# Expert stage of a transformer block: first two matrices behind the preceding third one, empty slots' rows out of bounds

## The chip, the cores and the metric

The kernel runs on one core of a Trainium2 chip. The metric is the device time of one execution in microseconds (us). TensorE is called PE, VectorE DVE, ScalarE ACT, GpSimd POOL; SyncE (SP) only issues transfers here.

## What is computed

A block with two attentions (not touched here) and a mixture of 32 experts over 512 tokens of width 1024, all in float32. Each token goes to two experts, so there are 1,024 rows of expert work. The part that matters, cut from the reference:

```python
top_v, top_i = lax.top_k(elog, TOP_K)                  # 2 experts for each token
yb = (silu(xc @ w1[e]) * (xc @ w3[e])) @ w2[e]         # w1, w3: 1024x512; w2: 512x1024
y = yb[dest] * sw[:, None]
out = segment_sum(y, stok, num_segments=T)             # a token's two rows are added
x = x + out
```

The weights w1, w3 and w2 of all experts are 32 x 3 x 2 MB = 201 MB, and each is read once.

## The kernel before

The expert stage (`moe`) handles the 32 experts as 16 pairs, p = 0 to 15. Each expert has 64 slots (`C`), so a pair fills the 128 partitions: the first expert has partitions 0 to 63, the second 64 to 127, and an expert's rows stand at the front of its 64 slots. The other slots are empty.

For one pair, `ffn` does this. PE multiplies the gathered tokens with w1 (32 matmul instructions, L1185) and with w3 (32 more). ACT takes the silu of the first result, DVE multiplies it by the second (L1203), PE transposes the product (4 instructions, L1205), ACT copies the transposed tile back (hT, L1208), and PE multiplies it with w2 (32 instructions, L1223, two blocks of 512 columns). ACT and DVE scale the two blocks into y by the router's weight, and POOL adds the 128 rows of y (4 KB each) into a buffer in HBM, obuf, by an indirect accumulating transfer (L1254). Its row numbers come from `slot_tables`: a filled slot names its token's row, 0 to 511; an empty slot on partition p names a row of its own behind them, 512 + p. obuf has 640 rows for that.

After each odd pair there is extra PE work for the next two pairs: small tables (16 instructions, L1154) behind w3, and the gathering of their tokens (64 instructions, L1050 and L1051) behind the transposes. `blocks`, some 20 small DVE instructions which prepare the rare overflow loop, is traced after pair 0 and shares the buffer tagged hg with silu's result.

The last pair is different: its w2 comes in blocks of 256 columns, and each block's rows are spread to the tokens by matmuls (pcb, L1245 and L1246) and added to X, the content of obuf, which POOL loads (L1318) into the two buffers that held w2's first two column blocks; then the result goes out.

Weights are loaded by SP alone (`load`, L898) in a fixed order, w1, w3, w2 of pair 0, then of pair 1, and so on, as transfers of 1 MB (198 transfers; the last pair's w2 comes in six of 512 KB and four of 256 KB). They land in a ring of 38 half-megabyte places, so transfer j can only be issued when transfer j-19 has been used up by PE, and a transfer that waits holds back all behind it.

PE's order is chosen by the scheduler when the kernel is built, within the dependencies and the orders written by hand. One of these is in `ffn`: from the middle of w1 (k = 4, `KF`) on, a pair's w1 goes behind the last w2 matmul of the pair before (`self.third`). The first half of w1, and w3, carry no such order. `self.third` is empty for pair 0 and set back in the overflow loop.

Of the kernel before, what the change touches and what calls it, by code (L numbers as in the profile page):

```python
# [20 lines left out]
mult, add, sub, eq = OP.mult, OP.add, OP.subtract, OP.is_equal  # L21

P = 128
T = 512
# [7 lines left out]
NEG = -1e30  # L32
NE = 32
EG = 8
KF = 4
C = 64
KS = 512
E0 = 8
# [31 lines left out]
class Kernel:  # L70
# [1033 lines left out]
    def moe(self):  # L1104
# [6 lines left out]
        def gather(base):  # L1111


            ns = base.shape[1]
            xT = wk.tile([P, KT, ns], F32, tag="xT", name="xT")
            sel = self.sel(ns)
            first = len(self.pgs) > 0
            for k2 in range(4):
                if first:
                    pg = self.pgs.pop(0)  # L1120
                else:
                    pg = ps.tile([P, 2, ns], F32, name="pg", tag="G", bufs=4)
                    for t in range(NT):
                        for k in (2 * k2, 2 * k2 + 1):
                            self.pick(pg, k, t, sel[t])
                for k in (2 * k2, 2 * k2 + 1):
                    src, gg = pg[:, k % 2, :], self.g2d[:, k:k + 1]
                    if k % 2:
                        s.activation(xT[:, k, :], src, AF.Copy, scale=gg)
                    else:  # L1130
                        v.tensor_scalar(xT[:, k, :], src, gg, None, op0=mult)
            return xT
# [5 lines left out]
        def token_rows(sel):  # L1138

            R = sel[0].shape[1]  # L1140
            sT = wk.tile([P, T], F32R, tag="sT", name="sT")
            pr = ps.tile([P, T], F32, name="pr", tag="Y")
            for t in range(NT):
                pe.transpose(pr[0:R, t * P:(t + 1) * P], sel[t].bitcast(F32), ident)
            s.copy(sT[0:R], pr[0:R])
            return sT
# [22 lines left out]
        def ffn(xT, cols, w, table, after=lambda: None, blocks=((0, 512), (512, 512)), sT=None, first=lambda: None, mid=lambda: None):  # L1169
# [8 lines left out]
            for name in ("w1", "w3"):  # L1178
                p = ps.tile([P, 512], F32, name="p" + name, tag="H")
                for k in range(KT):  # L1180
                    with ExitStack() as behind:
                        if name == "w1" and k == KF and self.third:
                            behind.enter_context(tc.issue_after(self.third))
                        for i in range(n):
                            end = pe.matmul(p[i * C:(i + 1) * C], xT[:, k, cols[i]], w(name, i, k),  # L1185
                                            start=k == 0, stop=k == KT - 1)
                after()
                ph.append(p)
# [27 lines left out]
            def outputs(c0, m):  # L1216
                o = c0 % 512
                if o == 0 and store:
                    y["h"] = wk.tile([P, 2, 512], F32R, tag="y" if c0 else "xT", name="yhl")
                p = ps.tile([P, m], F32, name="py", tag="Y")  # L1220
                for k in range(4):
                    for i in range(n):
                        e = pe.matmul(p[i * C:(i + 1) * C], hT[:, k, i * C:(i + 1) * C], w("w2", i, k, c0, m),  # L1223
                                      start=k == 0, stop=k == 3)
                self.third = e.ins
                if not store:
                    if c0:
                        e = v.tensor_scalar(yy[:, c0:c0 + m], p, ws, None, op0=mult)  # L1228
                    else:
                        e = s.activation(yy[:, c0:c0 + m], p, AF.Copy, scale=ws)  # L1230
                    self.evicted.append(e.ins)
                    return
                yh, yl = (y["h"][0:R, i, o:o + m] for i in range(2))
                s.activation(yh, p[0:R], AF.Copy, scale=ws[0:R])
                v.scalar_tensor_tensor(yl, p[0:R], ws[0:R], yh.bitcast(F32), op0=mult, op1=sub)
                return yh, yl
# [14 lines left out]
            if not store:  # L1251
                for b in blocks:
                    outputs(*b)
                g.indirect_dma_start(self.obuf, bass.IndirectOffsetOnAxis(ap=rows, axis=0), yy, None,  # L1254
                                     bounds_check=T + P - 1, compute_op=add)
                after()
                return
            done = None
# [8 lines left out]
        def overflow():  # L1267
# [3 lines left out]
            with tc.For_i(0, n, 1) as i:  # L1271
                e = nc.sync.value_load(oi[0:1, bass.ds(i, 1)], min_val=0, max_val=NE - 1)
                kb = wk.tile([P, 2], F32, tag="kb", name="kb")
                j = wk.tile([P, NB], F32, tag="kbj", name="kbj")
                v.scalar_tensor_tensor(j, iota16, self.octr, self.okey, op0=eq, op1=mult, accum_out=kb[:, 0:1])
                v.tensor_scalar(self.octr, self.octr, 1.0, None, op0=add)
                base = wk.tile([P, C], F32, tag="hg", name="obase")
                v.tensor_scalar(base, slot4[:, 0:C], kb[:, 0:1], -float((EG - 1) * KS), op0=add, op1=add)
                for t in range(NT):
                    self.select(t, base)  # L1280
                xT = gather(base)
                v.tensor_tensor(kb[:, 1:2], slotp, kb[:, 0:1], op=add)
                table, sT = slot_tables([(self.sel(C), kb[:, 1:2])])[0], token_rows(self.sel(C))

                ww, slot = {}, RA
                for name in ("w1", "w3", "w2"):
                    src = self.io[name][0][bass.ds(e, 1)].rearrange("o (p k) m -> p (o k m)", p=P)
                    for h in (0, 2):
                        t = self.ring1.tile([P, 2, 1024], F32, tag=f"w{slot}", name="wo")
                        nc.sync.dma_start(t.rearrange("p a b -> p (a b)"), src[:, 1024 * h:1024 * (h + 2)])  # L1290
                        ww[name, h], ww[name, h + 1] = t[:, 0], t[:, 1]
                        slot += 2

                def w(name, _, k, c0=0, m=512):
                    h, o = (k, c0) if name == "w2" else (k // 2, k % 2 * 512)
                    return ww[name, h][:, o:o + m]
                ffn(xT, (slice(0, C),), w, table, sT=sT)

        def pair_sel(p):
            c0 = p % 2 * 2 * C  # L1300
            return [x[:, c0:c0 + 2 * C] for x in self.sel(4 * C)]

        def tables(q):
            r = []
            for p in (2 * q, 2 * q + 1):
                kcol = wk.tile([P, 1], F32, tag="kcol", name="kcol", bufs=2)
                v.tensor_scalar(kcol, slotp, float(self.expert(p, 0) * KS), None, op0=add)
                r.append((pair_sel(p), kcol))
            return slot_tables(r)

        tabs, got, self.evicted, self.third = tables(0), [], [], None
        for p in range(NE // 2):
            last, odd = p == NE // 2 - 1, p % 2
            c0 = odd * 2 * C
            if last:
                self.X = [self.xpool.tile([P, 2, D], F32, tag=n, name="X") for n in ("c0", "c1")]
                for i, x in enumerate(self.X):
                    g.dma_start(x, self.obuf[2 * i * P:2 * (i + 1) * P].rearrange("(t p) m -> p t m", p=P))  # L1318
            elif odd:
                v.tensor_scalar(key, key, -float(KS), None, op0=add)  # L1320
                for t in range(NT):
                    self.select(t, slot4)

            def first():
                got.append(tables(p // 2 + 1))

            def mid():
                got.append(gather(slot4))
            ffn(xT, (slice(c0, c0 + C), slice(c0 + C, c0 + 2 * C)),
                lambda name, i, k, c0=0, m=512: self.weight(name, self.expert(p, i), k, c0, m), tabs[odd],  # L1330
                lambda: self.load(8), [(c, 256) for c in range(0, D, 256)] if last else ((0, 512), (512, 512)),
                token_rows(pair_sel(p)) if last else None, *((first, mid) if odd and not last else ()))
            if odd and not last:
                tabs, xT = got
                got.clear()
            if p == 0:
                self.blocks(ps, wk)
        overflow()

# [36 lines left out]
```

## Time and profile before

| | us |
|---|---|
| median of 3 runs | 1063.03 |
| lowest and highest | 1061.3, 1063.7 |
| profiled execution, its own time | 1062.07 |
| its span from first to last instruction | 1060.3 |
| PE busy | 965.3 |
| DVE, ACT, POOL busy | 478.4, 385.0, 229.9 |

The span is shown on the page in 40 slices of 26.5 us; a digit is a busy share in tenths. Attention fills the first half, the expert stage begins at about 555 us. "DMA share" is the mean busy share of the 16 DMA engines, and GB/s is what they moved. A row of the timeline gives start and duration in us, then engine, line, operation, names (out<-in), shape and count; in brackets the idle time before it and what ended it.

### The profile page before, as it was taken

To read this page: it belongs to the slowest core of one execution; us is meant where nothing else is said; L and a number is where in the kernel's file an instruction comes from. 1 tells how busy PE (TensorE), PEld (TensorE's weight loads), DVE (VectorE), ACT (ScalarE), POOL (GpSimd) and SP (SyncE) were. 2 spreads that over 40 slices of the span, in tenths; PEclk is the share of its full clock that TensorE was granted. 3 is DMA by queue.
4 is the path that set the end of the run, shared out by engine and by line. 5 is a ranking of instruction groups with operands and counts; after the bars stand their busy time and mean duration, and the time that the engine had idled before them with its cause. 6 is when DMAs were issued, how large, how long until landed. Compare 5 with 4: busy or idle time off the path is not lost.

```text
span 1060.3 us, 15524 instructions
## 1 busy us (share of the span) xinstructions
PE 965.3 (91%) x5718; PEld 682.9 (64%) x5718; DVE 478.4 (45%) x1469; ACT 385.0 (36%) x802; POOL 229.9 (22%) x378
## 2 busy tenths in 40 slices
PE   7799999999899999989999899999697987979886
PEld 7799989999678788879993535353262532626233
DVE  3868585574859889796471312112020120201002
ACT  5475565746856655654361111111010110101001
POOL 6444344314523232333230000000000000000000
PEclk9899999999999999999989899999898998989988
DMA  6322222112311211245879899999999999999995
GB/s 176 117 66 74 62 80 80 47 37 74 96 55 48 63 56 38 60 165 190 334 291 387 320 403 402 404 401 402 426 402 403 401 404 420 404 402 405 402 388 205
DMA packets 76510, 254.26 MB, mean 240 GB/s; under 512 B 11664, under 2 KB 46224, under 8 KB 52368
## 3 DMA queue, kind: packets, MB, share of 16 engines
q1 hardware_dynamic: 70304, 238.56, 57.9%
q0 software_dynamic: 2704, 9.96, 4.2%
q10 hardware_dynamic: 3424, 4.72, 1.2%
q8 instruction: 46, 0.75, 0.3%
q14 instruction: 32, 0.26, 0.1%
HBM read 240.64 MB, written 12.58 MB: 239 GB/s over the span
## 4 chain that ended last, share of the span: by engine, by line
PE 53%; DMA 31%; DVE 9%; ACT 3%; issue 1%; SPq 0%; POOL 0%; DVEq 0%; ACTq 0%; POOLq 0%
DMA w<-in_w_dram 29%; PE pw L1185 8%; PE py L1223 5%; PE pmm L92 5%; PE pmm L93 5%; PE pmm L94 5%; PE po L92 2%; PE po L94 2%; PE po L93 2%; PE pg L92 2%; PE pg L94 2%; PE pg L93 2%; PE pg L1050 2%; PE pg L1051 2%; PE pt L413 1%
## 5 line engine op out<-in xcount | busy, mean ns | idle before, releaser
L1185 PE MATMUL pw<-w,xT 128*64 128x512 f32 x1024 | 248.7, 611 | 46.9 <-DMA w<-in_w_dram 46.9
L314 POOL TENSOR_TENSOR wlo<-wraw,whi 128x256 fp32r<-128x256 f32 (+4 forms) x228 | 174.9, 799 | 219.1 <-ACT whi L312 208.8
L1185 PEld LDWEIGHTS pw<-w,xT 128*64 128x64 f32 x1024 | 83.2, 141 | 200.2 <-issue 185.1
L92 PE MATMUL pmm<-whi,hTh 128*128 128x256 f32 (+1 forms) x448 | 130.1, 293 | 3.7 <-ACT raw L480 2.6
L93 PE MATMUL pmm<-wlo,hTh 128*128 128x256 f32 (+1 forms) x448 | 130.1, 293 | 0.0
L94 PE MATMUL pmm<-whi,hTl 128*128 128x256 f32 (+1 forms) x448 | 127.4, 292 | 0.0
L1254 POOL DMA_INDIRECT obuf<-y,rows x15 | 23.5, 1570 | 455.3 <-DVE y L1228 455.3
L1223 PE MATMUL py<-w,hT 128*64 128x512 f32 x480 | 112.9, 603 | 1.4 <-ACT hT L1208 1.4
L1228 DVE TENSOR_SCALAR y<-py,ws 128x512 f32<-128x512 f32 x15 | 11.3, 751 | 191.1 <-PE py L1223 191.1
L1203 DVE TENSOR_TENSOR hg<-pw,hg 128x512 f32<-128x512 f32 (+1 forms) x19 | 16.4, 877 | 171.8 <-PE pw L1185 171.4
L92 PEld LDWEIGHTS pmm<-whi,hTh 128*128 128x128 f32 x448 | 85.5, 191 | 5.6 <-ACT raw L480 3.2
L93 PEld LDWEIGHTS pmm<-wlo,hTh 128*128 128x128 f32 x448 | 85.5, 191 | 2.0 <-issue 1.7
L94 PEld LDWEIGHTS pmm<-whi,hTl 128*128 128x128 f32 x448 | 84.1, 191 | 1.8 <-issue 1.7
L1223 PEld LDWEIGHTS py<-w,hT 128*64 128x64 f32 x480 | 37.4, 138 | 65.1 <-issue 61.3
L1208 ACT COPY hT<-pt 128x512 f32<-128x512 f32 x15 | 8.8, 586 | 178.7 <-PE pt L1205 178.7
L312 ACT CAST whi<-wraw 128x1024 fp32r<-128x1024 f32 (+4 forms) x70 | 64.7, 931 | 20.9 <-DMA wraw<-in_w_in_dram 6.7
L399 ACT ACTIVATE e<-pss,nm 128x128 f32<-128x128 f32 (+3 forms) x96 | 50.7, 531 | 49.8 <-DVE nm L395 36.9
L1050 PE MATMUL pg<-sel,hTh 128*128 128x256 f32 x256 | 65.7, 295 | 0.0
L1051 PE MATMUL pg<-sel,hTl 128*128 128x256 f32 x256 | 64.4, 290 | 0.0
L1200 ACT ACTIVATE hg<-pw 128x512 f32<-128x512 f32 x16 | 17.1, 1067 | 130.4 <-PE pw L1185 118.3
L395 DVE CUSTOM_DVE_ANT_0 pss<-pss,mask 128x128 f32<-128x128 f32 (+3 forms) x96 | 46.9, 496 | 18.4 <-PE pss L531 15.8
L92 PE MATMUL pg<-hTh,whi 128*128 128x512 f32 x128 | 50.8, 397 | 0.9 <-DVE cT L87 0.9
(349 smaller groups left out, 1902.4 us busy)
## 6 DMA issues: line engine op xcount, KB each, us to landing
w<-in_w_dram SPq DMA_DIRECT2D x188, 1024.0 KB, 21.3
wraw<-in_w_in_dram SPq DMA_DIRECT2D x38, 512.0 KB, 3.6
w<-in_w_dram SPq DMA_DIRECT2D x6, 512.0 KB, 11.3
wraw<-in_w_in_dram SPq DMA_DIRECT2D x8, 352.0 KB, 3.3
obuf<-X ACTq DMA_DIRECT2D x5, 512.0 KB, 10.8
wraw<-in_mla_w_ukv_dram SPq DMA_DIRECT2D x4, 512.0 KB, 4.2
wraw<-in_w_o_dram SPq DMA_DIRECT2D x4, 512.0 KB, 3.4
X<-in_x_dram SPq DMA_DIRECT2D x4, 512.0 KB, 5.0
```

The source lines that it names most:

```text
L92: self.pe.matmul(out, a[0], b[0], start=first, stop=False)
L93: self.pe.matmul(out, a[0], b[1], start=False, stop=False)
L94: self.pe.matmul(out, a[1], b[0], start=False, stop=last)
L312: s.copy(hi, raw)
L314: g.tensor_tensor(lo[:, k], raw[:, k], hi[:, k].bitcast(F32), op=sub)
L395: v.tensor_tensor_reduce(out=pss[:, 0:nk], in0=pss[:, 0:nk], in1=self.mask[:, 512 - nk:512], scale=-scale, scalar=3e38, op0=add, op1=OP.mi ...
L399: s.activation(e[:, 0:nk], pss[:, 0:nk], AF.Exp, scale=-1.0, bias=nm, accum_out=l[:, m:m + 1] if l0 is None or m else l0[qt])
L1050: self.pe.matmul(pg, self.h2h[:, t, k, :], sel, start=t == 0 and k % 2 == 0, stop=False, skip_group_check=True)
L1051: self.pe.matmul(pg, self.h2l[:, t, k, :], sel, start=False, stop=t == NT - 1 and k % 2 == 1, skip_group_check=True)
L1185: end = pe.matmul(p[i * C:(i + 1) * C], xT[:, k, cols[i]], w(name, i, k), start=k == 0, stop=k == KT - 1)
L1223: e = pe.matmul(p[i * C:(i + 1) * C], hT[:, k, i * C:(i + 1) * C], w("w2", i, k, c0, m), start=k == 0, stop=k == 3)
L1254: g.indirect_dma_start(self.obuf, bass.IndirectOffsetOnAxis(ap=rows, axis=0), yy, None, bounds_check=T + P - 1, compute_op=add)
```

## The change

Three edits. (1) The order by hand now holds from k = 0 on, and for w1 and w3 alike: a pair's first and second matrix go wholly behind the third of the pair before. (2) In the accumulating transfer the bound on row numbers is 511 in place of 639, and a number above it is no error: the rows of empty slots, 512 + p, are then out of bounds and left out. (3) `blocks` is traced after pair 1 in place of pair 0.

```diff
-KF = 4
@@ ffn
-                        if name == "w1" and k == KF and self.third:
+                        if k == 0 and self.third:
                             behind.enter_context(tc.issue_after(self.third))
@@ ffn, behind w2
                 g.indirect_dma_start(self.obuf, bass.IndirectOffsetOnAxis(ap=rows, axis=0), yy, None,
-                                     bounds_check=T + P - 1, compute_op=add)
+                                     bounds_check=T - 1, oob_is_err=False, compute_op=add)
@@ moe, loop over pairs
-            if p == 0:
+            if p == 1:
                 self.blocks(ps, wk)
```

## Rows read from the trace of the kernel before

**Rows 1.** The page's 40 slices: PE, DMA, rate.
```profile
PE   7799999999899999989999899999697987979886
...
DMA  6322222112311211245879899999999999999995
GB/s 176 117 66 74 62 80 80 47 37 74 96 55 48 63 56 38 60 165 190 334 291 387 320 403 402 404 401 402 426 402 403 401 404 420 404 402 405 402 388 205
```
**Rows 2.** A quiet window: engines' busy us, granted PE clock, DMA share, GB/s.
```profile
660.00:670.00 10.00, 10.00 (x57) 5.03 (x58) 4.02 (x12) 1.63 (x3) 0.00 (x0) 1.00 1.01 424
```
**Rows 3.** PE's waits, 557 to 1040 us: total us, times, longest.
```profile
PE pw L1185 <- DMA w<-in_w_dram: 46.9, 16, 9.2
PE pt L1205 <- DVE hg L1203: 5.4, 2, 4.2
PE py L1223 <- ACT hT L1208: 1.4, 2, 0.7
```
**Rows 4.** SP's waits, 440 to 1060 us: total us, times, longest.
```profile
SPq L898 <- DMA w<-in_w_dram: 336.4, 147, 4.6
SPq L898 <- PE py L1223: 31.5, 7, 14.5
```
**Rows 5.** PE's timeline, pairs 0 and 1.
```profile
557.11 17.39 PE L1185 MATMUL pw<-w,xT 128*64 128x512 f32 x80
574.43 0.66 PE L1205 MATMUL pt<-ident,hg 128*128 128x128 f32 x4
575.02 5.79 PE L1185 MATMUL pw<-w,xT 128*64 128x512 f32 x25
...
580.70 6.97 PE L1223 MATMUL py<-w,hT 128*64 128x512 f32 x30
...
599.64 1.12 PE L1205 MATMUL pt<-ident,hg 128*128 128x128 f32 x4 [4.16 <-DVE hg L1203]
```
**Rows 6.** Timeline of DVE, ACT and PE between w3 and w2 of pair 2.
```profile
631.10 1.06 DVE L1203 TENSOR_TENSOR hg<-pw,hg 128x512 f32<-128x512 f32 x1 [13.40 <-PE pw L1185]
...
634.67 0.59 ACT L1208 COPY hT<-pt 128x512 f32<-128x512 f32 x1 [9.72 <-PE pt L1205]
...
635.30 7.09 PE L1223 MATMUL py<-w,hT 128*64 128x512 f32 x32 [0.68 <-ACT hT L1208]
```
**Rows 7.** Windows around the hole in the transfers (columns as in rows 2).
```profile
576.00:583.00 7.00, 7.00 (x36) 2.54 (x34) 0.00 (x0) 0.00 (x0) 0.00 (x0) 1.00 0.92 382
583.00:590.00 7.00, 7.00 (x34) 2.60 (x30) 0.75 (x1) 0.69 (x1) 0.10 (x1) 1.00 0.35 118
...
595.00:601.00 6.00, 1.84 (x12) 1.75 (x12) 3.68 (x19) 1.25 (x2) 0.00 (x0) 0.67 1.04 328
601.00:608.00 7.00, 7.00 (x49) 7.00 (x49) 0.99 (x3) 1.33 (x3) 0.00 (x0) 0.79 1.01 427
```
**Rows 8.** The software DMA queue, 622 to 629 us: packets, MB, share of 16 engines.
```profile
q0 software_dynamic: 144, 0.52, 37.6%
```
**Rows 9.** PE's timeline, pairs 14 and 15.
```profile
1018.06 0.61 PE L1185 MATMUL pw<-w,xT 128*64 128x512 f32 x1 [1.77 <-DMA w<-in_w_dram]
...
1018.55 6.99 PE L1223 MATMUL py<-w,hT 128*64 128x512 f32 x30
...
1025.44 10.03 PE L1185 MATMUL pw<-w,xT 128*64 128x512 f32 x45
...
1038.85 2.81 PE L1223 MATMUL py<-w,free 128*64 128x256 f32 x24
```
**Rows 10.** SP's issue of the last 1 MB transfer, and landing times of it and its neighbours.
```profile
L898 SPq DMA_DIRECT2D w<-in_w_dram x1: 328/328/328, 1005.8 to 1005.8; - x1
...
DMA to landing us min/median/max: 18.6/19.1/19.6
```
**Rows 11.** Timeline of POOL and DVE: X at the end.
```profile
1041.96 1.54 POOL L1318 DMA_DIRECT2D X<-obuf  x2 [12.89 <-PE py L1223]
...
1047.45 1.29 DVE L1248 TENSOR_TENSOR X<-pcb,X 128x512 f32<-128x512 f32 x2 [1.69 <-DMA X<-obuf]
```

## The prediction

> **What bounds the kernel now.** I read the 40 slices first. The rate stands at 401 to 426 GB/s from slice 24 to slice 38, with the DMA engines at 9, while PE's digit drops to 6 and 7 in places [rows 1]. A quiet window gives the ceiling: 424 GB/s at a DMA share of 1.01 [rows 2]. So the expert stage runs at the pace of its weights. The waits say the same from both sides. PE waits for weights 16 times, 46.9 us in all [rows 3]; SP waits 336.4 us for its own earlier transfers, and only 31.5 us for places of w2 [rows 4]. Two places are not at that pace. Slices 20 to 23 hold 291, 387, 320 GB/s before the level is reached [rows 1]: there the ring is full and PE is late. And the last pair ends after its weights, as shown below. Anything saved in transfer time, in a hole of the transfers, or behind the last weight moves the end; what is saved or lost on PE in between does not, up to its waits.
>
>
> **The start: part 1, the order.** Before, PE does 80 matmuls in 17.39 us (w1 and w3 of pair 0, and 16 of pair 1's w1), the transposes, then 25 more of pair 1, and only then, to 587.7, pair 0's w2 [rows 5]. One matmul takes 17.39 / 80 = 0.217 us. The ring wants w2's places next: SP waits up to 14.5 us for them, the longest wait of all [rows 4], and the transfers have a hole. It costs (1 - 382/424) x 7 = 0.7 us in one window and (1 - 118/424) x 7 = 5.05 us in the next [rows 7], 5.7 us together.
> After the change w2 of pair 0 follows its own w1 and w3: 557.1 + 64 x 0.217 = 571.0; the multiplication, transposes and copy lie bare before it, 1.06 + 0.66 + 0.59 = 2.3 us [rows 5, 6]; 32 matmuls take 6.9 us. It ends at about 580.3, 7.3 us sooner, and the first places come free in its second half, at 579. The hole begins in the 576 to 583 window and holds until after 587, so it closes. Gain 5.7 us; the bounds are 0 (a later place is waited for instead) and 7.3.
>
> **The cover that is lost.** For each even pair the 2.3 us between w3 and w2 had matmuls of the next pair beside them (ahead of pair 2's w2 PE idled 0.68 us [rows 6]). Now PE stands still: 8 x 2.3 = 18 us at most. For odd pairs the tables and the gathering still lie there. Of the 18 us only pair 0's stands on the path (counted above); the others eat into 46.9 us of waiting [rows 3], so I cost them at nothing. Without that cover they cost 16 us. Behind w1 and w3, held back on PE's queue, wait silu and DVE's multiplication of the same pair, and SP's reuse of those places; w1's and w3's data arrive after w2's of the pair before in any case, so the new order is the order of arrival.
>
> **Part 2, the rows left out.** An accumulating transfer is 128 rows of 4 KB. Alone in a 7 us window, its queue shows 144 packets, 0.52 MB, 37.6% of the engines: 2.63 us of all 16 engines for one transfer [rows 8]. At 424 GB/s 0.52 MB would take 1.24 us, so an accumulating byte costs twice a plain one. There are 15 such transfers, 39.5 us. How many rows are empty: 1,024 rows of work over 16 pairs leave, for the first 15, about 960 of 1,920 slots; with the reference's router on its inputs I get 975 filled and 945 empty, 49.2%. If an empty row costs nothing and the rest spreads evenly, 15 x 2.63 x 0.492 = 19.4 us go. But a weight transfer has landed when its slowest engine is done, and filled slots stand at the front of each half of the partitions, so the engines may not be relieved alike; if one of them keeps all its rows, or if an empty row still makes its packet, nothing goes. No row of before shows which. Between 0 and 19.4 I take two thirds, 13 us: the average over engines is a row's figure, the loss to uneven sharing is not. That is 0.87 us for each transfer, 12.1 us for the 14 that lie ahead of the last pair's weights.
> [...]
> POOL's own time for the transfer isn't on the path; bounds 0.
>
> **Part 3, `blocks`.** It takes the buffer that silu of pair 1 wants: PE idles 4.16 us before pair 1's transposes [rows 5], and the clock falls to 0.67 and 0.79 for the 13 us around it [rows 7]. Behind pair 1 the DVE chain runs beside pair 2's w1 (6.9 us). It frees up PE at a time when the transfers are at their ceiling again (427 GB/s [rows 7]), so: nothing, bounds 0 and 4.
>
> **The end: part 1 once more.** Pair 14's w2 (30 matmuls from 1018.55) had to wait until 1018.06 for a first matmul on weights of pair 15, and then 45 matmuls of w1 and w3 run from 1025.44 to 1035.47 without a wait [rows 9]: PE is 10 us of work behind. The last of w3 was issued at 1005.8 and landed 18.6 to 19.6 us later, at about 1025 [rows 10]. In the new order pair 14's w2 is long done, and w3's second half, 16 x 0.217 = 3.5 us, ends at 1028.9 in place of 1035.5. From there on everything follows as before: two column blocks until 1041.66 [rows 9], then X is loaded into their places at 1041.96, and DVE adds from 1047.45 [rows 11]. Gain 6.6 us. Less: pair 14's accumulating transfer, which ran behind those weights, now comes ahead of them and delays them by what is left of it, 2.63 - 0.87 = 1.8 us. Net 4.8, bounds 0 (the clock falls behind a wait, as to 0.67 in a window with 4.16 us of it [rows 5, 7]; at half clock w3's second half takes 3.5 us more, and the rest likewise) and 6.6.
>
> **The sum**, against the profiled execution: 1062.07 - 5.7 - 12.1 - 4.8 = 1039.5. The median is 1.0 above that execution: 1040.
>
> **Rivals.**
> - *The rows are left out but no transfer time is.* Each empty row still makes a packet, or the fullest engine keeps all its rows. For it: filled rows stand close together. Against: the rows of one transfer are the only thing that its packets count. 1062.07 - 5.7 - (6.6 - 2.6) = 1052.4, so 1053 as a median.
> - *Only the rows count.* The order gives back what it gains: another place of the ring is waited for at the start, and X or the last column blocks bind at the end. For it: X's data is waited for, 1.69 us [rows 11]. 1062.07 - 13.0 = 1049.1, so 1050.
> - *PE becomes the bound (slower).* Every pair, not only the even ones, has a bare stretch, and the clock falls behind each as it did after the 4.16 us [rows 7]: 2.3 us plus some 2.2 us at half clock, 4.5 x 15 = 67.5 us, against 46.9 + 5.4 + 1.4 = 53.7 us that PE idles now [rows 3]; 1062 + 13.8 = 1076. It decides from 53.7 / 15 = 3.6 us a pair on. Against: odd pairs keep 9 us of other work there, and behind the gap of 0.68 us 32 matmuls took 7.09 us, full pace [rows 6].
> - *No difference*: hole, rows and tail all give back; 1063.
>
> **How the numbers follow.** Forecast 0.60, with its own range of 1030 (all of the 19.4 saved, 7.3 at the start) to 1046. No transfer time saved 0.22; only the rows 0.09; PE bound 0.06; no difference 0.03. The range takes in the first three: from 1029 to 1054, the 1053 with a little room. Faster by over 0.2% (2.1 us, about what a measurement of this kernel can tell from no change) are the first three, 0.91; within it 0.03; slower 0.06.
>
> **What would show each step.** After: no 118 GB/s window near 585, and no wait of SP for w2 of over 10 us; w2 of pair 0 ending near 580. The software queue with about 15 x 65 rows in place of 1,920, and its share of the engines near 2.5% in place of 4.2%; if the packets fall but the weights' pace between pairs doesn't, the engines are not relieved alike. PE's waits for weights in more and shorter pieces, and bare gaps of 2 to 3 us at even pairs only. At the end, w3's last matmul 3 to 4 us behind its landing. Wrong I would be above all if the queue's packets stay at their number, or if PE's waits vanish.

## The result, and the profile after

The changed kernel takes 1037.93 us (median of 4, 1036.11 to 1039.05) beside 1062.76 us of the kernel before on the same chip: 24.8 us less, ratio 0.9766 with a 95% interval of 0.9746 to 0.9785. The forecast was 1040. The profiled execution has 1039.05 us and a span of 1037.3 us.

The page's slices (25.9 us each), and its two main DMA queues (packets, MB, share of the 16 engines):

```profile
PE   7799999999989999999999999999998897987985
...
DMA  6422222122322112153697999999999999999996
GB/s 175 124 62 63 82 82 69 42 58 69 84 62 64 56 42 61 31 190 122 250 380 282 408 412 411 423 405 421 415 410 417 409 412 407 426 411 411 413 362 235
...
q1 hardware_dynamic: 70304, 238.56, 59.6%
q0 software_dynamic: 2704, 6.10, 2.5%
```

Against [rows 1] the level of 405 GB/s and more is reached at slice 23 (counted from 1) and holds to slice 38 without a hole, and PE's digit is 9 from slice 13 to 30. The software queue moves 6.10 MB; the page of before has 2704 packets, 9.96 MB and 4.2%. So the packets stay at their number, 3.86 MB go (945 rows of 4 KB are 3.87 MB), and 1.7% of the span, 18 us of all 16 engines.

Waits of PE (557 to 1040 us) and of SP (440 to 1060 us), to be read beside [rows 3, 4]: total us, times, longest.

```profile
PE pw L1184 <- DMA w<-in_w_dram: 17.1, 9, 3.6
PE pt L1204 <- DVE hg L1202: 9.6, 8, 1.2
PE py L1222 <- ACT hT L1207: 5.4, 8, 0.7
PE py L1222 <- DMA w<-in_w_dram: 3.1, 3, 1.3
...
SPq L897 <- DMA w<-in_w_dram: 295.6, 135, 4.3
SPq L897 <- PE py L1222: 39.2, 14, 13.3
SPq L897 <- PE pw L1184: 36.1, 20, 5.5
```

PE waits 20.2 us for weights where it waited 46.9, and stands bare in 8 pairs for 9.6 + 5.4 = 15.0 us: the cover that the even pairs lost. SP still waits up to 13.3 us for w2's places, but the transfers already issued cover that now. The start shows it (PE's timeline, then windows with columns as in [rows 7]):

```profile
557.78 13.95 PE L1184 MATMUL pw<-w,xT 128*64 128x512 f32 x64
572.96 0.66 PE L1204 MATMUL pt<-ident,hg 128*128 128x128 f32 x4 [1.22 <-DVE hg L1202]
574.29 8.78 PE L1222 MATMUL py<-w,hT 128*64 128x512 f32 x32 [0.68 <-ACT hT L1207]
...
576.00:583.00 7.00, 7.00 (x32) 2.21 (x30) 0.00 (x0) 0.69 (x1) 0.00 (x0) 0.86 1.01 421
583.00:590.00 7.00, 7.00 (x36) 2.35 (x34) 0.75 (x1) 0.00 (x0) 1.84 (x1) 1.00 1.00 401
```

In place of 80 + 25 matmuls ahead of pair 0's w2 [rows 5] there are 64, and 583 to 590 us holds 401 GB/s where it held 118. At the end (timeline of PE, issue and landing of the last 1 MB transfer, POOL and DVE; beside [rows 9 to 11]):

```profile
1003.47 8.78 PE L1184 MATMUL pw<-w,xT 128*64 128x512 f32 x30 [2.32 <-DMA w<-in_w_dram]
...
L897 SPq DMA_DIRECT2D w<-in_w_dram x1: 328/328/328, 987.6 to 987.6; - x1
...
DMA to landing us min/median/max: 20.9/20.9/20.9
...
1018.74 1.52 POOL L1317 DMA_DIRECT2D X<-obuf  x2 [22.75 <-DMA w<-in_w_dram]
1024.43 1.29 DVE L1247 TENSOR_TENSOR X<-pcb,X 128x512 f32<-128x512 f32 x2 [1.90 <-DMA X<-obuf]
```

The last of w3 lands at 987.6 + 20.9 = 1008.5 and PE's last matmul on it ends at 1003.47 + 8.78 = 1012.25, 3.8 us later; before it was 1035.5 against about 1025, 10 us. From there to the end of the span it is 25.0 us, before 24.8.

### The profile page after: what moved, and what is told of

It reads as the page before. It is cut to its first block, busy times and chain, and to the rows that moved or that the text cites. A ratio compares the mean times of both kernels' runs of the same rounds, so it can differ in the third digit from the quotient of the medians.

```text
span 1037.3 us, 15532 instructions
## 1 busy us (share of the span) xinstructions
PE 962.0 (93%) x5718; PEld 676.7 (65%) x5718; DVE 477.3 (46%) x1469; ACT 385.3 (37%) x802; POOL 230.1 (22%) x378
## 3 DMA queue, kind: packets, MB, share of 16 engines
q0 software_dynamic: 2704, 6.10, 2.5%
## 4 chain that ended last, share of the span: by engine, by line
PE 49%; DMA 33%; DVE 11%; ACT 4%; issue 2%; SPq 0%; POOL 0%; DVEq 0%; ACTq 0%; POOLq 0%
DMA w<-in_w_dram 30%; PE pw L1184 7%; PE pmm L91 5%; PE pmm L92 5%; PE pmm L93 5%; PE py L1222 4%; PE po L93 2%; PE po L91 2%; PE po L92 2%; PE pg L91 2%; PE pg L93 2%; PE pg L92 2%; PE pg L1049 2%; PE pg L1050 2%; PE pt L412 1%
## 5 line engine op out<-in xcount | busy, mean ns | idle before, releaser
L1184 PE MATMUL pw<-w,xT 128*64 128x512 f32 x1024 | 236.2, 604 | 17.1 <-DMA w<-in_w_dram 17.1
L1184 PEld LDWEIGHTS pw<-w,xT 128*64 128x64 f32 x1024 | 78.7, 139 | 168.3 <-issue 132.2
L1222 PEld LDWEIGHTS py<-w,hT 128*64 128x64 f32 x480 | 34.9, 139 | 76.5 <-issue 60.8
## 6 DMA issues: line engine op xcount, KB each, us to landing
w<-in_w_dram SPq DMA_DIRECT2D x188, 1024.0 KB, 20.2
```

## Experiments

Two theories on the rows left out were to be told apart: the pace of the weights follows the engine with most filled rows (A), or the mean of the engines (B). A needs a rule by which rows go to engines; no trace here shows one, so any split named below is an assumption. And each part of the sum was to be measured alone. Times are medians; the kernel before, in the same job, had 1063.63 us for the first four, 1062.38 for the next four and 1061.76 for the last four.

A second measure is the expert stage alone, from PE's first matmul on w1 of pair 0 to the end of the span, in the one profiled execution of each kernel. That first matmul comes between 557.1 and 560.0 us, and the times can carry this spread, though the order and the rows are changed only behind it. The changed kernel, e8 and e11 turn out to be one program, and their stages agree within 0.1 us.

| kernel | stage, us |
|---|---|
| before | 503.2 |
| changed, e8, e11 | 479.5, 479.5, 479.4 |
| e1, e2 | 493.8, 490.0 |
| e3 and e12 (one kernel), e4 | 476.9 and 476.5, 494.0 |
| e5, e6, e7 | 479.7, 484.5, 485.1 |
| e9, e10 | 495.4, 477.0 |

### The order alone, the rows alone

```diff
 # e1: the changed kernel
-bounds_check=T - 1, oob_is_err=False, compute_op=add
+bounds_check=T + P - 1, compute_op=add
 # e2: the kernel before
-bounds_check=T + P - 1, compute_op=add
+bounds_check=T - 1, oob_is_err=False, compute_op=add
```

> The new order and the moved blocks alone; empty rows are added to rows of their own, as before. Theory (hole at the start 5.7 us, end 6.6 less the 2.6 of pair 14's transfer): 1062.8 - 9.7 = 1053, with 1,920 full rows in the software queue. Rival (only the rows count): 1062 to 1063.

Measured: 1053.89, 9.7 us less than before, ratio 0.9915 (0.9892 to 0.9937). The order is worth what the sum had for it without the rows, 5.7 + 4.0 (9.4 by the stage).

> The old order, blocks behind pair 0, only the empty rows out of bounds. [...] Theory B (the mean over the 16 engines counts): 1062.8 - 18.7 = 1044. Hole of the transfers near 585 us and PE's backlog at the end as in the kernel before.

Measured: 1049.51, 14.1 us less, ratio 0.9877 (0.9855 to 0.9900), 13.2 by the stage. That is less than B's 18.7. The hole stays: in this kernel's windows (columns as in [rows 7]) 583 to 590 us holds 108 GB/s.

```profile
583.00:590.00 7.00, 7.00 (x35) 2.65 (x31) 0.75 (x1) 0.69 (x1) 0.04 (x1) 1.00 0.37 108
```

9.7 + 14.1 = 23.8 us beside the 24.8 of both (by the stage 22.6 beside 23.7): the parts add up.

### The same rows on other partitions

```diff
 # e3 and e12: positions dealt to the columns in turn, four columns to a group
-g.iota(self.slot4, pattern=[[EG * KS, 4], [1, C]], base=E0 * KS, ...)
 # (the two lines that filled self.slotp go as well)
+for i in range(4):
+    g.iota(self.slot4[:, i * C:(i + 1) * C], pattern=[[32, 2], [1, 8], [8, 4]], base=(E0 + EG * i) * KS, ...)
 # self.slotp, the slot number by partition, is read off the same table
+v.scalar_tensor_tensor(self.M.rearrange("p t e -> p (t e)"), self.slot4[:, 0:P], 1.0, self.ident, op0=mult, op1=mult, accum_out=self.slotp)
 # e4: packed; the same with
+    pattern=[[4, 2], [8, 8], [1, 4]]
```

Position n of an expert goes to column 32*(n div 32) + 4*(n mod 8) + (n div 8) mod 4 of its 64 in e3, and to 32*((n div 4) mod 2) + 4*(n div 8) + n mod 4 in e4.

> [...] The number of rows, and all work, is the same. [...] Theory A with another split (row number mod 16): 82 in place of 76 rows, 2 us more, 1040. Theory B (mean over the engines): no difference, 1038.

> [...] Same rows, same work. [...] Theory A with row number mod 16: 82 rows, 1040. Theory B (mean): no difference, 1038.

Measured: spread 1036.84, ratio 0.9745 (0.9721 to 0.9769); packed 1053.20, ratio 0.9911 (0.9891 to 0.9931). Packed takes back the whole of what the rows gave: it is as slow as e1, which leaves no row out. Both kernels leave out the same rows and bytes, so theory B falls, and so does a split by row number mod 16 (1040).

To see the rule without the router's numbers, two kernels left out 64 rows of each transfer by partition:

```diff
-bass.IndirectOffsetOnAxis(ap=rows, axis=0)
+bass.IndirectOffsetOnAxis(ap=self.rconst, axis=0)
 # e9:  rconst[p] = p for partitions 0 to 63,             512 + p for the others
 # e10: rconst[p] = p for partitions 0 to 31 and 64 to 95, 512 + p for the others
```

> The changed kernel with row numbers that don't come from the router: in each accumulating transfer partitions 0 to 63 are added to rows 0 to 63 and partitions 64 to 127 are left out, so the additions go to the wrong tokens. 64 of 128 rows are left out each time, about as many as in the changed kernel (63). [...] Theory B (the mean over the engines counts): 1037 as in the changed kernel.

> As e9, but partitions 0 to 31 and 64 to 95 are added (to rows of the same number) and the other 64 left out. [...] Theory A with blocks of 8 partitions to an engine: nothing is saved, 1053. Theory B: 1037, as e9.

Measured: e9 1056.68 (its runs lie between 1051.52 and 1058.11), ratio 0.9935 (0.9912 to 0.9958); e10 1036.47, ratio 0.9755 (0.9731 to 0.9779). Twenty microseconds (18.4 by the stage) lie between two kernels with the same number of rows left out. B had 1037 for both and falls with e9; A with blocks of 8 partitions to an engine had 1053 for e10 and falls with it. By the stage e9 saves nothing against e1 (495.4 beside 493.8) and e10 16.8 us, where half of the rows' time, 15 x 2.63 / 2 [rows 8], would be 19.7. In the stretch from 640 to 960 us, the issues of 1 MB transfers (count, then duration, then first and last start) and the software queue, in turn for e1, the changed kernel, e4, e9 and e10:

```profile
L897 SPq DMA_DIRECT2D w<-in_w_dram x118: 327/328/328, 639.9 to 958.2; - x118
q0 software_dynamic: 1584, 5.77, 9.0%
```

```profile
L897 SPq DMA_DIRECT2D w<-in_w_dram x122: 327/328/384, 641.1 to 959.0; - x122
q0 software_dynamic: 1584, 3.06, 4.9%
```

```profile
L896 SPq DMA_DIRECT2D w<-in_w_dram x117: 327/328/385, 641.3 to 958.5; - x117
q0 software_dynamic: 1584, 3.06, 4.9%
```

```profile
L902 SPq DMA_DIRECT2D w<-in_w_dram x117: 327/328/328, 642.6 to 959.5; - x117
q0 software_dynamic: 1584, 2.89, 4.7%
```

```profile
L902 SPq DMA_DIRECT2D w<-in_w_dram x123: 327/328/385, 640.9 to 958.6; - x123
q0 software_dynamic: 1584, 2.89, 4.7%
```

Last start less first, over the count less one, is the time for one transfer: 318.3 / 117 = 2.72 us in e1; 2.63 in the changed kernel; 2.73 in e4 and 2.73 in e9, no better than e1 although their queue moves half as much; 2.60 in e10. These windows cut pairs in the middle. Over ten whole pairs (120 transfers, from the landing of the 61st to that of the 181st) it is 2.70, 2.64, 2.72, 2.70 and 2.61 us for the same five kernels. From the landing of the 25th, before the first accumulating transfer, to that of the 188th, the last of 1 MB, e1 takes 444.2 us, the changed kernel 429.5, e4 444.1, e9 445.8 and e10 426.9: the differences in the stage arise there. In e4 and e9, which save nothing, rows 32 partitions apart are kept together (0 and 32, 1 and 33, and so on); in e10 never. Which engine a row goes to no trace shows.

The landing signals in the traces of the kernel before and of the changed one agree with engines that are relieved unevenly. Each weight transfer gives 16, as many as there are engines, and counts as landed with the last. For transfers issued ahead of the first addition (at 571.5 and 581.8 us) the 16 come within 0.5 us in both kernels. For those issued at 959 us they come within 3.6 us in the kernel before, which adds all rows, and within 15.7 us in the changed kernel. That fits A: what counts is the engine that is relieved least.

How much does the spreading give? e3 and the changed kernel were run once more side by side:

> The changed kernel as it is, beside the others on one chip, so that small differences to it can be read. Every theory: 1038, ratio to the kernel before 0.977.

> The kernel of e3 beside the changed kernel on one chip. Theory A: 2 to 4 us less than it, about 1035. Theory B: the same.

Measured: 1039.73, ratio 0.9787 (0.9768 to 0.9806), and 1036.83, ratio 0.9758 (0.9737 to 0.9778): 2.9 us, the intervals just overlapping. In the first jobs it was 0.9766 and 0.9745. By the stage it is 2.9 us here and 2.6 in the first jobs, clear of the 0.1 us between the changed kernel's three stages. Spreading wins 2 to 3 us; apart from e10, which does not add to the tokens' rows, it is the fastest version here.

The landing times in the traces tell it pair by pair. In the changed kernel 39, 63, 41 and 83 of the 128 rows are left out in pairs 10 to 13 (packets of 8 bytes in its trace); the second experts of these pairs have 57, 36, 38 and 25 rows. The twelve weight transfers that land around each of these four additions (from the 133rd landing to the 181st) take 32.2, 32.1, 32.1 and 31.1 us; in e1 they take 32.2, 32.1, 32.1 and 32.4, in e10, with 64 rows left out each time, 31.0, 31.1, 31.1 and 31.1. So in pairs 10 to 12 nothing is saved, although 39 to 63 of the 128 rows are left out: 63 in pair 11 give nothing where 64 in e10 give 1.0 us. Pair 8, whose second expert has 37 rows and where 47 are left out, does not go with these three: 31.7 us, and 32.7 in e1.

### Which pairs the order pays for

In both kernels the new order holds for one pair, and `blocks` is behind pair 0.

```diff
 # e2, with
-if name == "w1" and k == KF and self.third:
+if self.third and (k == 0 if self.strict else name == "w1" and k == KF):
 # e6: self.strict = p == 1        e7: self.strict = p == 15
```

> The kernel before with the empty rows left out (e2, 1049.5), and the new order for one pair alone: w1 and w3 of pair 1 behind w2 of pair 0. Theory: the hole of the transfers near 585 closes, 5.7 us, about 1044; PE's backlog at the end stays. Rival (the places are only waited for later, the hole moves): 1049.5.

> As e6, but the new order for the last pair alone: w1 and w3 of pair 15 behind w2 of pair 14. Theory: PE's backlog of 6.6 us at the end goes, less about 1.8 us for pair 14's transfer, which moves ahead of the last weights: 1049.5 - 4.8 = 1044.7; the hole near 585 stays. Rival (X or the last column blocks bind): 1049.5.

Measured: e6 1046.24, ratio 0.9846 (0.9829 to 0.9862); e7 1044.40, ratio 0.9830 (0.9814 to 0.9845). Against e2's 0.9877 that is 3.3 and 5.0 us, each with some 3 us of uncertainty; by the stage it is 5.5 and 4.9 (e6's stage began 2.8 us later than e2's). The windows show the hole closed in the first and open in the second:

```profile
583.00:590.00 7.00, 7.00 (x38) 2.32 (x36) 2.44 (x14) 0.00 (x0) 1.84 (x1) 1.00 1.00 401
```

```profile
583.00:590.00 7.00, 7.00 (x36) 2.74 (x33) 0.75 (x1) 0.69 (x1) 0.00 (x0) 1.00 0.31 80
```

By the stage the rows, pair 1 and pair 15 make 13.2 + 5.5 + 4.9 = 23.6 of 23.7 us: two pairs of sixteen account for what the order gives, and in the others it neither gains nor costs anything that these runs can tell.

### The small parts

```diff
 # e5: the changed kernel
-if p == 1:
+if p == 0:
     self.blocks(ps, wk)
 # e8: the changed kernel
-if k == 0 and self.third:
+if name == "w1" and k == 0 and self.third:
```

> The changed kernel with blocks traced behind pair 0 again. Theory (what it costs falls beside w1 of the next pair, as the order keeps them apart): no difference, 1038, and no wait of PE's transposes of over 1.3 us. Rival (the 4.2 us wait of the kernel before comes back and stands on the path): 1042.

> The changed kernel with w1 behind the third from its first matmul on, but w3 without that order. Theory (w3 fills the stretch before w2 and holds it up just as w1's half did): the hole (5.7 us) comes back, since 32 matmuls of w3 take 6.9 us, and so does a backlog at the end of up to 7 us: 1044 to 1051. Rival (w1's half alone did the harm): 1038.

Measured: e5 1040.42, ratio 0.9800 (0.9781 to 0.9819); e8 1038.89, ratio 0.9777 (0.9757 to 0.9797). In e5 the long wait of PE does not come back; PE's waits for DVE, 557 to 1045 us, are those of the changed kernel:

```profile
PE pt L1204 <- DVE hg L1202: 9.7, 8, 1.2
```

Its profiled span is 1037.3, the same as the changed kernel's; no difference is shown. For e8 the expectation missed: nothing came back. The scheduler makes the same program of both kernels, so e8 is the changed kernel once more, and the order on w3 is idle here: with w1 held back, the scheduler does not put w3 ahead of it.

## Why the prediction was right

**The bound.** Right (the slices with 291, 387 and 320 GB/s are 21 to 23, not 20 to 23). What relieved the transfers moved the end: the level without a hole, and the time per transfer, from 2.70 us (e1) to 2.64 over ten whole pairs.

**The start, 5.7.** The mechanism is shown (64 matmuls ahead of w2 in place of 105, 401 in place of 118 GB/s, and e6 against e7). By times it is worth 3.3 us, with 5.7 within the uncertainty, by the stage 5.5. One term was missing: pair 0's w2 took 8.78 us, not 6.9; the granted clock was 1.00 from 557 to 574.3 us, 0.55 from 574.3 to 578.1 (0.50 from 576 to 577) and 1.00 from there to 583.1, so part of it ran at about half of the clock before. The bare 1.22 and 0.68 us ahead of it are not enough to explain that: behind the same two gaps w2 of pairs 2, 4 and 6 took 7.09 us. Why the clock fell here is open. w2 ended at 583.1 instead of the 580.3 that I had worked out (0.7 of that because pair 0 began later). The transfers in flight covered it.

**The rows, 13 of 0 to 19.4.** 14.1 measured (e2), 13.2 by the stage. The two thirds were a choice between ends and happened to be near; the reason that I gave for the loss, engines relieved unevenly, fits e4, e9 and e10, and the landing signals (16 within 15.7 us where it was 3.6). The even share, 19.4, came out high. From the landing of the 25th transfer to that of the 61st, with the additions of pairs 0 to 2 and 209 rows left out, the changed kernel gains 6.6 us on e1; from there to the 181st, with pairs 3 to 13 and 675 rows left out, 6.9. Why the first pairs gain more is not settled.

**Lost cover, at no cost.** Right: 15.0 us of bare waits at even pairs for the 18 at most, against 26.7 us less waiting for weights, and outside pairs 1 and 15 the order cost nothing that can be told (23.6 of 23.7 us above).

**`blocks`, nothing.** Not contradicted (e5). Its 4.16 us wait had needed the old order as well: in e6, with `blocks` behind pair 0 and the new order for pair 1 alone, PE's longest wait for DVE before the transposes is 1.2 us, in e7 4.2.

**The end, 4.8.** 5.0 by times (e7), 4.9 by the stage, and w3's last matmul 3.8 us behind its landing for the 3.5 forecast.

**What the signs said.** Three were wrong though the steps behind them held. I took the software queue's packets for the count of rows, though [rows 8] has 144 for 128 rows, and named their staying as the clearest sign against me; they stayed at 2,704, but 945 of them carry no row any more, as the bytes and the share (2.5%, as forecast) show. SP still waits 13.3 us for a place of w2, where I had wanted no wait of over 10. And PE's waits for weights became fewer, not more: 12 pieces in place of 16, and shorter, 3.6 us at most in place of 9.2.

**The rivals.** No transfer time saved: e4 and e9 have it, at 1053 and 1057, where the filled rows are packed or stand on partitions 0 to 63. Only the rows count: falls with e1, where the order alone gives 9.7 us. PE as the bound: falls, as PE still waits 20.2 us for weights, and stands bare for 15.0 us in all, in the even pairs alone.

## What to carry to other kernels

Where transfers are the bound, issue the consumer's work in the order in which its data arrive, and look for it at the two ends of the stage: where the ring first fills and behind the last load. Leaving 64 of 128 rows out of each transfer saved nothing here where partitions 0 to 63 stayed (e9), and 16.8 us by the stage where 0 to 31 and 64 to 95 did (e10), so look at which partitions stay before counting bytes. A hand-made order should be checked against what the scheduler does without it: here the half of it on w3 changed no instruction.

## What the runs showed of the hardware that was not expected

A row out of bounds, with the error off, still makes a packet in the indirect accumulating transfer: 144 packets for one transfer as in [rows 8], but 0.27 MB and 17.7% of 8 us, 1.42 us of all engines in place of 2.63. In the trace of the changed kernel the packet of an empty row has 8 bytes and takes 9 ns; that of a filled row has 4 KB and takes 327 ns, where a weight packet of 8 KB takes 309 (medians). The changed kernel's software queue, 618 to 626 us:

```profile
q0 software_dynamic: 144, 0.27, 17.7%
```

And the mean DMA share hardly tells e9 from e10: over 640 to 960 us it is 1.01 in the one and 1.02 in the other (windows of the two in turn, columns as in [rows 2]), although the weights come at 2.70 and 2.61 us a transfer.

```profile
640.00:960.00 320.00, 289.13 (x1446) 128.77 (x1444) 48.44 (x145) 33.85 (x51) 17.11 (x11) 0.97 1.01 400
640.00:960.00 320.00, 295.41 (x1550) 137.76 (x1548) 52.51 (x159) 36.37 (x56) 16.13 (x11) 0.99 1.02 412
```
